# A hybrid decoder block: 14 of 24 gate tiles computed as pairs in one-level Strassen form

## The chip, the cores and the metric

The kernel runs on one core of a Trainium2 chip. Its parts are TensorE (PE, matrix products, which write to the accumulator memory PSUM), VectorE (DVE), ScalarE (ACT), GpSimd (POOL), and DMA engines; every transfer here is issued by SyncE (SP), which works through its list in order, as each engine does. The metric is the device time of one execution in microseconds (us), median of several runs. A profile, the "trace", was taken of one more execution.

## The reference

The work is one block of a decoder with D = 1024 features and 1024 tokens, 16 meta tokens prepended. Shortened:

```python
u = rms_norm(h, norm_mix)
qa, ka, va, qf, kf, vf, fl, xc, yc, gates = split(u @ w_in)
o_a = swa_sink_attention(qa, ka, va, ...)     # 8 heads, window of 128
o_f = forgetting_attention(qf, kf, vf, ...)   # 8 heads, causal, bias from cumulated log_f
o_c = rg_lru(causal_depthwise_conv(xc), ...) * gelu(yc)
g = sigmoid(gates).reshape(b, t, 3, D)
merged = g[..., 0, :] * (o_a @ w_branch[0]) + g[..., 1, :] * (o_f @ w_branch[1]) \
       + g[..., 2, :] * (o_c @ w_branch[2])
h = h + merged @ w_out
h = h + (silu(gate_ff) * up_ff) @ w_ffn_out   # gate_ff, up_ff from rms_norm(h) @ w_ffn_in
out = rms_norm(h)[16:]
```

`gates` has 3 x 1024 columns: 24 tiles of 128 features, each for 1024 tokens.

## The kernel before

All matrix products work on numbers split in two parts, `hi` and `lo` (`split`: ACT writes `hi`, DVE writes `lo` = source minus `hi`), and each product is three matmuls: hi*hi, hi*lo, lo*hi (`mm3`, L151). So one gate tile is 2 token halves x 8 blocks of 128 features x 3 = 48 matmuls with 512 columns. Its weights (512 KB) are loaded into a tile `wr` and split into `wh` and `wl`; each half's sum is copied from PSUM by ACT into a tile `z` and stored to the DRAM buffer `gz` (`gate`, L733).

The stages, in order of time:

1. Norm of the input, which leaves `uh` and `ul` (u, features in partitions), and the first projections.
2. The recurrence (`lru`, L359): 4 blocks of 128 channels, mostly long DVE and ACT operations and a scan. Beside it PE works on the remaining projections of the recurrence and on the values of both attentions (`values`, `mm_v`, results `vst`).
3. The attentions: first the sliding window (`swa_scores`, `swa_values`), then the forgetting one (`fox_scores`, `fox_values`). Scores go from PSUM (`sc`) through DVE (bias and maximum), ACT (exponential), DVE (reciprocal) and POOL (scaling; in the sliding window, every other tile on DVE, L596) to PE for transposes (`tr`), through `split` (`ph`, `pl`), and to PE again for the product with the values (`ob`).
4. The branch products (`mm_br`) of mixers A and C, from `o` tiles loaded from the DRAM buffer `osp`, with `gz` through a sigmoid (`sg`); then branch F; then the output projection.
5. The SwiGLU and its output, already in one-level Strassen form: 7 products instead of 8 on half-size blocks, with sums of blocks built by `combine` (L999) and `swiglu` (L943).

The order in stages 2 and 3 is made by `drive` (L237): a `side` generator (recurrence, or attention) yields after each piece, and between two pieces a `main` generator is stepped until its matmuls, at a written cost of 2.4 columns per ns and 3 ns each, add up to a gap: `LRU_GAP` = 3500 ns in the recurrence, `GAPS` = 850 ns in the sliding window, 480 ns in the forgetting attention. What is saved up is capped at `CREDIT` gaps. A scheduler then places the instructions of each engine. `main` beside the attentions holds the q and k projections and all 24 gates; what is left of them when the attention ends is done after it, alone. In time, the recurrence's last block runs beside the first projections of the attention.

Tiles live in pools on two sides of the on-chip memory; a pool that is opened after another was closed takes its place, and a tile waits for the last use of the one it lies on. Tiles of one tag rotate over a given number of buffers (`wh` and `wl` have two each).

## Time and profile before

| | |
|---|---|
| median of 3 runs | 1651.43 us (1650.43 to 1652.25) |
| the profiled execution | 1652.01 us, of which the span is 1650.2 |
| instructions in the span | 22634 |
| DMA | 242.48 MB, mean 147 GB/s |
| recurrence, from its first DVE operation to its last | 52.66 to 233 us of the span |
| attentions, first scores in a row to the last `ob` | about 240 to 734 us |
| gates after the attention | 734.41 to 777 us |

The span is one execution as the profiler saw it; the execution's own time is 1.8 us longer. PE is busy nearly all the time, but a matmul's busy time contains that of its neighbours, since they are pipelined. What PE really can do is read from how far apart matmuls start where nothing holds them up.

### The profile page before, as it was taken

To read this page: it belongs to the slowest core of one execution; us is meant where nothing else is said; L and a number is where in the kernel's file an instruction comes from. 1 tells how busy PE (TensorE), PEld (TensorE's weight loads), DVE (VectorE), ACT (ScalarE), POOL (GpSimd) and SP (SyncE) were. 2 spreads that over 40 slices of the span, in tenths; PEclk is the share of its full clock that TensorE was granted. 3 is DMA by queue.
4 is the path that set the end of the run, shared out by engine and by line. 5 is a ranking of instruction groups with operands and counts; after the bars stand their busy time and mean duration, and the time that the engine had idled before them with its cause. 6 is when DMAs were issued, how large, how long until landed. Compare 5 with 4: busy or idle time off the path is not lost.

```text
span 1650.2 us, 22634 instructions
## 1 busy us (share of the span) xinstructions
PE 1627.5 (99%) x8159; PEld 1372.3 (83%) x8159; DVE 1006.8 (61%) x1815; ACT 759.7 (46%) x1397; POOL 389.4 (24%) x322
## 2 busy tenths in 40 slices
PE   7999999999999999999999999999999999999998
PEld 6899978888888888888887888888888788888886
DVE  6566566555566666651338446977776777466554
ACT  6466466555555555542335443433333343355342
POOL 2000001011122221110224100267765667300000
PEclk9999999999999999999999999999999999999999
DMA  7222342223324142329747221344554444698632
GB/s 254 78 103 94 131 139 77 95 82 122 108 75 129 63 123 73 115 98 318 252 142 230 96 90 70 127 156 172 198 202 148 147 149 151 214 359 275 191 128 102
DMA packets 110880, 242.48 MB, mean 147 GB/s; under 512 B 11944, under 2 KB 23544, under 8 KB 110512
## 3 DMA queue, kind: packets, MB, share of 16 engines
q1 hardware_dynamic: 110768, 241.04, 43.0%
q8 instruction: 64, 1.05, 0.3%
q14 instruction: 48, 0.39, 0.1%
HBM read 163.45 MB, written 72.21 MB: 143 GB/s over the span
## 4 chain that ended last, share of the span: by engine, by line
PE 81%; DVE 6%; DMA 4%; POOL 3%; issue 3%; ACT 2%; SPq 0%; DVEq 0%; POOLq 0%; ACTq 0%
PE mm_w L151 27%; PE mm_s L151 7%; PE mm_br L151 6%; PE mm_wo L151 5%; PE mm_x L1147 4%; PE mm_v L151 4%; PE tr_s L151 4%; PE tr_y L1147 4%; PE sc_y L1147 4%; PE ob L547 4%; PE tr L558 3%; DMA wr<-w_fi_dram 2%; PE sc_s L151 2%; PE ob_x L1147 1%; PE mm_g L151 1%
## 5 line engine op out<-in xcount | busy, mean ns | idle before, releaser
L151 PE MATMUL mm_w<-uh,wh 128*128 128x512 f32 (+2 forms) x744 | 292.6, 393 | 0.0
L151 PE MATMUL mm_w<-uh,wl 128*128 128x512 f32 (+2 forms) x744 | 280.6, 377 | 0.0
L151 PE MATMUL mm_w<-ul,wh 128*128 128x512 f32 (+2 forms) x744 | 279.9, 376 | 0.0
L151 PEld LDWEIGHTS mm_w<-uh,wl 128*128 128x128 f32 x744 | 140.0, 188 | 25.7
L151 PEld LDWEIGHTS mm_w<-uh,wh 128*128 128x128 f32 x744 | 140.4, 189 | 12.8
L151 PEld LDWEIGHTS mm_w<-ul,wh 128*128 128x128 f32 x744 | 140.7, 189 | 11.7
L119 DVE TENSOR_TENSOR ab<-raw,ab 128x1024 fp32r<-128x1024 f32 x77 | 92.9, 1223 | 71.5 <-ACT ab L118 62.0
L118 ACT ACTIVATE wh<-wr 128x1024 fp32r<-128x1024 f32 (+1 forms) x84 | 72.0, 858 | 125.3 <-PE mm_w L151 52.3
L118 ACT ACTIVATE ab<-raw 128x1024 fp32r<-128x1024 f32 x77 | 80.8, 1059 | 95.0 <-PE ob_x L1147 21.4
L151 PE MATMUL mm_s<-pt,ar 128*128 128x512 f32 x492 | 118.8, 390 | 0.8 <-ACT c L954 0.7
L151 PE MATMUL mm_br<-o,wh 128*128 128x512 f32 x384 | 118.3, 389 | 0.0
L119 DVE TENSOR_TENSOR pl<-tr,ph 128x384 fp32r<-128x384 f32 (+2 forms) x160 | 87.4, 555 | 46.9 <-ACT ph L118 42.7
L151 PEld LDWEIGHTS mm_s<-pt,ar 128*128 128x128 f32 x492 | 92.0, 188 | 21.5 <-ACT c L968 1.3
L118 ACT ACTIVATE ph<-tr 128x384 fp32r<-128x384 f32 (+2 forms) x160 | 77.0, 486 | 52.9 <-PE tr L558 50.9
L119 DVE TENSOR_TENSOR wl<-wr,wh 128x1024 fp32r<-128x1024 f32 x45 | 55.8, 1241 | 73.4 <-ACT wh L118 73.1
L648 POOL TENSOR_SCALAR s<-s,sm 128x144 f32<-128x144 f32 (+3 forms) x64 | 48.8, 765 | 171.0 <-DVE sm L647 138.1
L151 PEld LDWEIGHTS mm_br<-o,wh 128*128 128x128 f32 x384 | 72.1, 188 | 14.8
L558 PE MATMUL tr<-ident,s 128*128 128x128 f32 x480 | 79.6, 274 | 1.2 <-POOL s L596 0.6
L151 PE MATMUL mm_wo<-woh,hl 128*128 128x512 f32 x256 | 79.1, 389 | 0.0
L151 PE MATMUL mm_br<-o,wl 128*128 128x512 f32 x192 | 75.2, 392 | 1.5 <-DVE wl L119 1.5
L558 PEld LDWEIGHTS tr<-ident,s 128*128 128x128 f32 x480 | 59.1, 140 | 18.3 <-DVE pl L119 3.4
L1147 PE MATMUL mm_x<-ab 128*128 128x512 f32 x297 | 72.7, 389 | 0.0
(258 smaller groups left out, 3651.9 us busy)
## 6 DMA issues: line engine op xcount, KB each, us to landing
wr<-w_in_dram SPq DMA_DIRECT2D x45, 512.0 KB, 3.6
wr<-w_fi_dram SPq DMA_DIRECT2D x44, 512.0 KB, 4.1
raw<-asp SPq DMA_DIRECT2D x77, 256.0 KB, 3.3
asp<-a SPq DMA_DIRECT2D x66, 256.0 KB, 2.8
gz<-z SPq DMA_DIRECT2D x48, 256.0 KB, 2.0
o<-osp SPq DMA_DIRECT2D x24, 512.0 KB, 5.9
sg<-gz SPq DMA_DIRECT2D x48, 256.0 KB, 3.5
fo<-w_fo_dram SPq DMA_DIRECT2D x22, 512.0 KB, 4.5
```

Of the source, the lines that this page charges most:

```text
L118: a = act.activation(hi, src, AF.Copy)
L119: i = dve.tensor_tensor(lo, src, f32(hi), ALU.subtract)
L151: pe.matmul(ps, a, b, start=first and i == 0, stop=i == n - 1, skip_group_check=not first)
L547: pe.matmul(ob[:, q0:q0 + b - a], vt[:, c], x[:, a:b], start=count == 0, stop=count == n_mm - 1, skip_group_check=True)
L558: pe.transpose(tb[:, col:col + P], src, ident)
L648: pool.tensor_scalar(s[:, :nk], s[:, :nk], den, 1.0, ALU.mult, ALU.mult)
L1147: pe.matmul(banks[x], a[:, 0, q], b[:, 1], start=first and j == 0 and c == 0, stop=j == NJ - 1 and c % 3 == 2, skip_group_check=True)
```

## The change

- Three gates stay plain and move into the recurrence's stage (`PLAIN`), one behind the values of the second set, two at the end. The recurrence's pieces come at shorter gaps (`LRU_GAP` 2200), and the projections of its last block move ahead of the values.
- A new stage follows the recurrence: `combine` builds four sums T1 to T4 of the quarters of u (`ub`: 2 feature halves x 2 token halves, so each quarter and each sum is two tiles of 128 x 1024), in the space that the recurrence leaves (`rt`, with three scratch tiles `fo` in `rf`).
- Seven pairs of gate tiles (`gate_pair`, `PAIRS`) are then computed in 7 products of 12 matmuls instead of 96 matmuls. Each pair needs 7 splits of 128 x 512, 4 sums of weight blocks, and 3 copies and 3 additions of partial results. Its tiles (`rg`) take the place of `rf`.
- Seven gates remain beside the attentions. `GAPS` are 290 and 345 ns, `CREDIT` is 30, and a gate can be interrupted by a q or k projection.
- In the sliding window all of the scaling is on POOL.
- The branch products run in the order A0, A1, C0, A2, C1, ... instead of A0, C0, A1, C1, ...
- `sub`, `add`, `product`, `operand` and `combine` move up in the file; `combine` takes its tiles as arguments.

```diff
-LRU_GAP = 3500.0
-GAPS = (850.0, 480.0)
-CREDIT = 8
+LRU_GAP = 2200.0
+GAPS = (290.0, 345.0)
+PLAIN, PAIRS = 3, 7
+CREDIT = 30
...
+    def combine(blocks, pair, temp):
+        b11, b21, b12, b22 = blocks
+        t3, t2, t1 = ([pair(i) for _ in range(2)] for i in (3, 2, 1))
+        room = lambda: temp().rearrange("p (k t) -> p k t", k=2)
+        v2 = []
+        for i in range(2):
+            v3 = room()
+            v2.append(room())
+            for v, x, y in zip((v3, v2[i]), b22[i], b12[i]):
+                sub(dve, v, f32(x), f32(y))
+            add(dve, v3, v3, v2[i])
+            for x, y in zip((v3, v2[i]), b11[i]):
+                add(dve, v2[i], x, f32(y))
+            split(*t2[i], v2[i])
+            split(*t3[i], v3)
+        def less_t2(t, b):
+            for i in range(2):
+                v = room()
+                sub(dve, v, f32(b[i][0]), v2[i])
+                add(dve, v, v, f32(b[i][1]))
+                last = split(*t[i], v)
+            return last
...
     def lru_main():
...
+        yield from proj(XC + 3, FULL, xs)
+        yield from proj(YC + 3, REAL, ys)
+        done.add(("lru", 3))
         yield from values(1, w_v1, 328)
...
-        yield from proj(XC + 3, FULL, xs)
-        yield from proj(YC + 3, REAL, ys)
-        done.add(("lru", 3))
+        yield from gate(gates.pop(0))
...
         yield from values(0, w_v0, 320)
+        for _ in range(PLAIN - 1):
+            yield from gate(gates.pop(0))
...
+        rt = ctxg.enter_context(tc.tile_pool(name="rt", bufs=1, side="right", reuse_waits="tile"))
+        with tc.tile_pool(name="rf", bufs=1, side="right", reuse_waits="tile") as rf:
+            ub = [[tuple(x[c][:, k:k + 2, (0 if c else NM):(0 if c else NM) + 512] for x in (uh, ul))
+                   for k in (k0, k0 + 2)] for c in range(2) for k0 in (0, 4)]
+            ub, _, rest = combine(ub, lambda i: [rt.tile([P, D], F32R, tag="t", bufs=16, name=nm("t"))
+                                                 .rearrange("p (k t) -> p k t", k=2) for _ in range(2)],
+                                  lambda: rf.tile([P, D], F32, tag="fo", bufs=3, name=nm("fo")))
+            ub.append(rest())
+    rg = ctxg.enter_context(tc.tile_pool(name="rg", bufs=1, side="right", reuse_waits="tile"))
+
+    def gate_pair(ja, jb, pl):
+        b11, b21, b22, t1, t2, t3, t4 = ub
...
+        product(p1, operand(wp, "wh", 2, a11), b11)
+        act.activation(c11, p1, AF.Copy)
+        product(p2, operand(wp, "wl", 2, a12), b21)
+        add(dve, c11, p2, c11)
+        dma(gz[ja, :, lo], c11)
+        sub(dve, a21, a11, a21)
+        sub(dve, s2, a22, a21)
+        product(p1, operand(rg, "ar", 3, s2), t2, False)
+        act.activation(c12, p1, AF.Copy)
+        add(dve, a11, s2, a11)
+        product(p5, operand(rg, "ar", 3, a11), t1)
+        act.activation(c22, p5, AF.Copy)
+        product(p1, operand(rg, "ar", 3, a21), t3, False)
+        add(dve, c22, p1, c22)
+        dma(gz[jb, :, hi], c22)
+        sub(dve, a12, a12, s2)
+        product(p5, operand(wp, "wh", 2, a12), b22, False)
+        add(dve, c12, p5, c12)
+        dma(gz[ja, :, hi], c12)
+        product(p1, operand(wp, "wl", 2, a22), t4, False)
+        act.activation(c21, p1, AF.Copy)
+        dma(gz[jb, :, lo], c21)
+
+    for i in range(PAIRS):
+        gate_pair(gates.pop(0), gates.pop(0), rg if i % 2 else wp)
+    ctxg.close()
...
-                (dve if jj % 2 else pool).tensor_scalar(s4[:, jj, lo:], ...)
+                pool.tensor_scalar(s4[:, jj, lo:], s4[:, jj, lo:], sm[:, 1, jj:jj + 1], 1.0, ALU.mult, ALU.mult)
...
-        todo = [(g, m) for m in range(8) for g in (0, 2)]
+        todo = [(0, 0), (0, 1)] + [(g, m + d) for m in range(8) for g, d in ((0, 2), (2, 0)) if m + d < 8]
```

How the change moves instructions is seen in the order that the built programs have, engine by engine. A row is line, operation, output<-inputs and shape; no times are in it.

First DVE behind the last values (`vst`). Before, the recurrence's last block (`g`, `q`, `x`, `y`, `xl`) alternates with the first k and q projections:

```order
L119 TENSOR_TENSOR wl_2109<-wr_2106,wh_2108 128x1024
L393 TENSOR_TENSOR g_1818<-g_1818,x_1803 128x1040
L396 SCALAR_TENSOR_TENSOR q_1849<-r_1817,q_1849 128x1040
L119 TENSOR_TENSOR k_1942<-mm_w_256_2007,k_1941 64x512
L397 TENSOR_TENSOR g_1818<-q_1849,g_1818 128x1040
L492 SCALAR_TENSOR_TENSOR q_2040<-mm_w_262_2048,q_2040 64x512
L400 SCALAR_TENSOR_TENSOR x_1856<-r_1817,g_1818 128x1040
L492 SCALAR_TENSOR_TENSOR q_2041<-mm_w_262_2048,q_2041 64x512
L401 SCALAR_TENSOR_TENSOR y_853<-x_1856,y_853 128x1024
L492 SCALAR_TENSOR_TENSOR q_2040<-mm_w_263_2077,q_2040 64x512
L119 TENSOR_TENSOR wl_2303<-wr_2300,wh_2302 128x1024
L119 TENSOR_TENSOR xl_1860<-y_853,xh_1859 128x1024
```

In the change the recurrence's operations are over by the last `vst`, and 26 operations of 128 x 1024 follow, the sums and splits of `combine` (`fo`, `t`). These are the last eight of them and what comes next, the first operand (`ar`) for a product that needs a sum of u:

```order
L370 TENSOR_TENSOR fo_2098<-fo_2098,ul_102 128x1024
L120 TENSOR_TENSOR t_2070<-fo_2098,t_2069 128x1024
L367 TENSOR_TENSOR fo_2107<-uh_99,fo_2072 128x1024
L370 TENSOR_TENSOR fo_2107<-fo_2107,ul_101 128x1024
L367 TENSOR_TENSOR fo_2112<-uh_99,fo_2083 128x1024
L120 TENSOR_TENSOR t_2104<-fo_2107,t_2103 128x1024
L370 TENSOR_TENSOR fo_2112<-fo_2112,ul_101 128x1024
L120 TENSOR_TENSOR t_2106<-fo_2112,t_2105 128x1024
L367 TENSOR_TENSOR s_293_2132<-wr_2124 128x512
L370 TENSOR_TENSOR c_2129<-sc_w_288_2127,c_2129 128x512
L370 TENSOR_TENSOR wr_2122<-s_293_2132,wr_2122 128x512
L120 TENSOR_TENSOR ar_2169<-s_293_2132,ar_2169 128x512
```

So the block of weights `s`, the addition into `c` and the operand `ar` of the first pair, which lie in `rg` on the space of `fo`, stand behind all of `combine`. On ACT the same stretch begins like this (`z` are copies of the plain gates' sums, `mm_w` their banks, `wh` and `wl` here the first pair's operands):

```order
L484 ACTIVATE z_1958<-mm_w_250_1933 128x512
L119 ACTIVATE wh_2134<-wr_2122 128x512
L484 ACTIVATE z_1986<-mm_w_252_1961 128x512
L119 ACTIVATE wl_2150<-wr_2122 128x512
L119 ACTIVATE t_2063<-fo_2072 128x1024
L119 ACTIVATE t_2059<-fo_2071 128x1024
L484 ACTIVATE z_2020<-mm_w_257_1995 128x512
L119 ACTIVATE t_2065<-fo_2083 128x1024
```

The first `hi` part of a sum (`t`) now stands behind copies of the plain gates' halves and behind the pair's `wh` and `wl`.

Second, SP behind the attention. Before, the loads of mixer C's `o` tiles and then of the first branch weights (`wb`) and gates (`sg`) alternate with the stores of the gates that PE does alone; two more of these come behind `wb`:

```order
L58 DMA gz<-z_7730 128x512
L58 DMA o_1431_7846<-osp 128x1024
L58 DMA o_1435_7850<-osp 128x1024
L58 DMA o_1432_7847<-osp 128x1024
L58 DMA gz<-z_7758 128x512
L58 DMA o_1436_7851<-osp 128x1024
L58 DMA wb_7876<-w_br_dram 128x512
L58 DMA sg_7878<-gz 128x512
L58 DMA sg_7879<-gz 128x512
L58 DMA wb_7882<-w_br_dram 128x512
L58 DMA gz<-z_7792 128x512
L58 DMA sg_7884<-gz 128x512
```

In the change only two stores of such gates are left here, `wb` comes behind the last of them and five more `o` loads:

```order
L59 DMA gz<-z_7918 128x512
L59 DMA o_1474_7970<-osp 128x1024
L59 DMA o_1478_7974<-osp 128x1024
L59 DMA o_1475_7971<-osp 128x1024
L59 DMA gz<-z_7946 128x512
L59 DMA o_1479_7975<-osp 128x1024
L59 DMA o_1476_7972<-osp 128x1024
L59 DMA o_1480_7976<-osp 128x1024
L59 DMA o_1477_7973<-osp 128x1024
L59 DMA o_1481_7977<-osp 128x1024
L59 DMA wb_8002<-w_br_dram 128x512
L59 DMA sg_8004<-gz 128x512
```

Third, PE in the sliding window. Before, matmuls of a gate (`mm_w`) stand in groups of three and four between transposes (`tr`) and products with the values (`ob`):

```order
L558 MATMUL tr_2279<-ident,s_2154 128x128 x3
L558 MATMUL tr_2310<-ident,s_2154 128x128 x4
L151 MATMUL mm_w_320_2372<-uh_100,wl_2303 128x512
L151 MATMUL mm_w_320_2372<-uh_100,wh_2302 128x512
L151 MATMUL mm_w_320_2372<-ul_102,wh_2302 128x512
L151 MATMUL mm_w_320_2372<-uh_100,wl_2303 128x512
L547 MATMUL ob_2278<-ph_2280,v_2117 128x128
L151 MATMUL mm_w_320_2372<-uh_100,wh_2302 128x512
L151 MATMUL mm_w_320_2372<-ul_102,wh_2302 128x512
L558 MATMUL tr_2333<-ident,s_2154 128x128
L547 MATMUL ob_2278<-pl_2281,v_2117 128x128
```

In the change fewer of them stand between the scores (`sc`) and the rest; from the first scores of the sliding window to the last `ob` of the forgetting attention, the order has 1342 matmuls `mm_w` of 512 columns before, and 660 in the change. From that last `ob` to the first `mm_br` it has 189 before and 105 in the change.

```order
L707 MATMUL sc_3771<-k_3057,q_3439 128x256
L670 MATMUL ob_3696<-pl_3726,v_3235 128x128
L708 MATMUL sc_3771<-k_3058,q_3439 128x256
L152 MATMUL mm_w_551_3753<-ul_101,wh_3749 128x512
L152 MATMUL mm_w_551_3753<-uh_99,wl_3750 128x512
L707 MATMUL sc_3788<-k_3057,q_3439 128x256
L708 MATMUL sc_3788<-k_3058,q_3439 128x256
L152 MATMUL mm_w_551_3753<-uh_99,wh_3749 128x512
L152 MATMUL mm_w_551_3753<-ul_101,wh_3749 128x512
L152 MATMUL mm_w_551_3753<-uh_99,wl_3750 128x512
L707 MATMUL sc_3805<-k_3057,q_3439 128x256
L708 MATMUL sc_3805<-k_3058,q_3439 128x256
```

More of the change, by code (lines that the diff above doesn't have):

```diff
@@ L418, in lru_side, with gate, zsink @@
             yield from lru(m, bdh, bdl)
+    gates = [8 * g + m for g in (0, 2, 1) for m in range(8)]
+    def gate(j):
+        def zsink(ps, n, t0):
+            zt = zp.tile([P, 512], F32, tag="z", bufs=2, name=nm("z"))
+            act.activation(zt, ps[:, :n], AF.Copy)
+            dma(gz[j, :, t0:t0 + n], zt)
+        yield from proj(GT + j, REAL, zsink)
     def lru_main():
@@ L747, in main @@
                     done.add(key)
+                    continue
+                part_of = part_of or gate(gates.pop(0))
+                cost = next(part_of, None)
+                if cost is None:
+                    part_of = None
                 else:
[L749 removed]
+                    yield cost
         drive(main(), side(), lambda: GAPS[mixer[0]])
```

121 lines of the change are left out of this document (51 added, 70 removed).

## The prediction

> **What bounds the kernel now.** I read the page first: busy shares, then the chain of waits that ended last.
>
> ```profile
> PE 1627.5 (99%) x8159; PEld 1372.3 (83%) x8159; DVE 1006.8 (61%) x1815; ACT 759.7 (46%) x1397; POOL 389.4 (24%) x322
> PE 81%; DVE 6%; DMA 4%; POOL 3%; issue 3%; ACT 2%; SPq 0%; DVEq 0%; POOLq 0%; ACTq 0%
> ```
>
> TensorE sets the end: it is busy 99% of the span and holds 81% of the chain. How much time a matmul really takes is read from that chain in order of time (start, length, what), where PE runs without a break:
>
> ```profile
> 734.41 42.88 PE mm_w L151 x189
> 777.30 86.83 PE mm_br L151 x383
> 1303.00 2.72 PE sc_s L151 x12
> ```
>
> 42.88 / 189 and 2.72 / 12 both give 0.227 us for a matmul of 512 columns; the first line is also the gates that PE does alone behind the attention, and `mm_br` follows them at once. A saved matmul is worth 0.227 us as long as PE has its next operands in time; where it has not, nothing of the saving is seen. So everything below is a comparison of what PE has left to do at a place with what the others need until then. The busy time by stages (start:end, length, then PE, its weight loads, DVE, ACT, POOL, the clock, the DMA share and GB/s) tells how much cover there is:
>
> ```profile
> 240.00:426.50 186.50, 185.38 (x1017) 156.75 (x1016) 108.29 (x290) 100.72 (x259) 22.47 (x35) 1.00 0.27 93
> 426.50:734.40 307.90, 306.85 (x1831) 266.06 (x1830) 195.31 (x620) 168.99 (x353) 64.61 (x77) 1.00 0.31 95
> 734.40:777.30 42.90, 42.90 (x191) 35.49 (x190) 5.11 (x7) 10.00 (x15) 0.00 (x0) 1.00 0.92 320
> ```
>
> Beside the attentions DVE is busy 304 of 494 us, so the gates there hide it easily. In the 43 us behind them the DMA is the busy one: 92%, 320 GB/s.
>
> **The change, part by part.** *Fewer matmuls.* Seven pairs need 84 instead of 96 matmuls each: 84 fewer, 84 x 0.227 = 19.0 us. This is the whole gain; nothing else is removed from PE. Within the pairs PE should run as in the SwiGLU's same products (2.72 us each, above): a pair is 19.0 us of PE, against 14 DVE operations of 128 x 512 at 0.60 (rows below), 8.4 us, and 10 on ACT at 0.63, 6.3 us. Hidden.
>
> *The sums of u.* The recorded order of DVE has 26 operations of 128 x 1024 behind the last `vst`, and the operand of the first pair's third product behind all of them. The SwiGLU's own sums show their price (start, length, engine; then one split on ACT and one of the values):
>
> ```profile
> 1046.96 0.69 DVE L119 TENSOR_TENSOR ar<-s,ar 128x512 fp32r<-128x512 f32 x1
> 1047.56 1.22 DVE L900 TENSOR_TENSOR fo<-pt,fo 128x1024 f32<-128x1024 f32 x1
> 1048.70 1.22 DVE L119 TENSOR_TENSOR pt<-fo,pt 128x1024 fp32r<-128x1024 f32 x1
> ...
> 1039.36 1.06 ACT L118 ACTIVATE pt<-fo 128x1024 fp32r<-128x1024 f32 x1 [4.11 <-DVE fo L903]
> ...
> 184.60 0.49 DVE L119 TENSOR_TENSOR vst<-mm_v,vst 128x320 fp32r<-128x320 f32 x1 [3.41 <-ACT vst L118]
> ```
>
> From start to start 1.14 us for 1024 columns, 0.60 for 512; ACT's half of a split takes 1.06. Count from the end of the last `mm_v`. PE then has two plain gates (96 matmuls) and the two products that need only u itself (24): 120 x 0.227 = 27.2 us. DVE needs about 1 us for the last `vst` (ACT's copy, then 0.49), 26 x 1.14 = 29.6, and seven operations of 512 among and behind them, 4.2: 34.8 us, were it never to wait. It waits, though. The pair's `wh` can be written only when the first plain gate's `wh` is free, after 48 matmuls, at 10.9; DVE stands before its half of it at 1 + 6 x 1.14 = 7.8, and ACT does `wh`, a copy, `wl` and the first sum's `hi` (some 3 us) before DVE has its first half of a sum, at about 14 instead of 9; that is some 4.6 lost. And four of the eight splits of sums have nothing of DVE's between the sum and its `lo`, so DVE stands for ACT's 1.06 to 1.2 each: 4.6. That makes 44.0, and PE, ready at 27.2, waits 17 us. Bounds: 7.6 if DVE never waits, 19 if its dependent operations take 1.22 instead of 1.14. I take 17, since buffers and order force the waits. Behind PE's third product stand all its later ones and the attention; nothing else can be issued.
>
> *Behind the attention.* PE has 105 matmuls there instead of 189, 23.8 us. SP's own queue in this stretch before, two groups of DMA issues (size, time to landing), and on ACT the last copy of a gate and the first split of a branch weight:
>
> ```profile
> 737.12 0.32 SPq L58 DMA_DIRECT2D osp<-pl  x1
> ...
> 738.03 0.40 SPq L58 DMA_DIRECT2D o<-osp  x1
> ...
> 761.69 0.32 SPq L58 DMA_DIRECT2D gz<-z  x1
> 762.05 1.41 SPq L58 DMA_DIRECT2D o<-osp  x3
> ...
> 767.97 0.44 SPq L58 DMA_DIRECT2D wb<-w_br_dram  x1
> ...
> o<-osp SPq DMA_DIRECT2D x18, 512.0 KB, 5.9
> wb<-w_br_dram SPq DMA_DIRECT2D x4, 256.0 KB, 5.3
> ...
> 771.94 0.60 ACT L736 ACTIVATE z<-mm_w 128x512 f32<-128x512 f32 x1 [4.84 <-PE mm_w L151]
> 774.37 0.63 ACT L118 ACTIVATE wh<-wb 128x512 fp32r<-128x512 f32 x1 [1.83 <-DMA wb<-w_br_dram]
> ```
>
> The loads start 3.6 us after the last `ob` (734.4) and the first `wb` is there at 774.3, 40 us after it; PE came at 777.1. With 23.8 us of cover, the same loads cannot be done. In the change's order SP first waits for the last plain gate's copy (24.4 with ACT's 0.6), issues its store (0.32), five more `o` loads at 0.47, and `wb`: 27.1. With 5.3 us to land and 0.63 for the split, PE starts at 33.1 instead of 23.8: a wait of 9.3. By the load instead: 16 x 0.524 + 5 x 0.262 of `gz` + 0.524 of `w_out` + 0.262 = 10.5 MB at 320 GB/s is 32.8, from 3.6 on, and 0.63: 37.0, a wait of 13.2. If `wb` lands in 2 us, 6.0. I take 9.5, near the queue's own walk. The order A0, A1 lets mixer C's tiles come 5.4 us later, but `wb` stands behind them all the same. The Trainium skill, "DMA: Bandwidth & Descriptors", section "Where 436 GB/s comes from", says that HBM transfers are bound by about 358 GB/s per core; an estimate by it is 29.3 us for these bytes and a wait of 9.7. This trace ran at 320 in this stretch.
>
> *A restart after a long wait.* At its start PE had idled, and its first matmuls came slowly:
>
> ```profile
> 15.90 0.43 PE L151 MATMUL mm_w<-uh,x1h 128*128 128x272 f32 x1
> ...
> 17.76 0.43 PE L151 MATMUL mm_w<-ul,x0h 128*128 128x272 f32 x1
> 17.99 0.43 PE L151 MATMUL mm_w<-uh,x0l 128*128 128x272 f32 x1
> ...
> 19.35 0.31 PE L151 MATMUL mm_w<-uh,x0l 128*128 128x272 f32 x1
> ...
> 19.87 0.29 PE L151 MATMUL mm_w<-uh,x0h 128*128 128x272 f32 x1
> 19.99 0.29 PE L151 MATMUL mm_w<-ul,x0h 128*128 128x272 f32 x1
> ```
>
> 0.23 apart until 19.35 and 0.12 from there: 3.45 us at half the pace, 1.7 lost. Whether a wait in the middle does the same no row shows, because there is none so long; 0 to 1.7 for each of the two new waits. I take 1.7, the only row of a PE that had stood long: 3.4. The Trainium skill's page "TensorE: Matmul & The Clock Gate", section "What's actually happening", says that after an idle window of about 3.4 us the array runs at half rate until it was busy as long again; by it the term stays, without it it is 0.
>
> *A denser attention.* From the first scores to the last `ob` the order has 660 wide `mm_w` instead of 1342: 154.6 us of cover go elsewhere, and 494 us become 340 if nothing stalls. DVE loses 15 of its splits of gate weights and half of the scaling (groups of DVE: count | busy, mean ns | idle before and what ended it; the first of the forgetting attention, the others of the sliding window; last a wait of the chain):
>
> ```profile
> L119 DVE TENSOR_TENSOR wl<-wr,wh 128x1024 fp32r<-128x1024 f32 x18 | 22.1, 1225 | 36.1 <-ACT wh L118 36.1
> L596 DVE TENSOR_SCALAR s<-s,sm 128x256 f32<-128x256 f32 x32 | 12.9, 442 | 0.5
> L119 DVE TENSOR_TENSOR pl<-tr,ph 128x512 fp32r<-128x512 f32 x15 | 10.4, 691 | 12.7 <-ACT ph L118 12.5
> L119 DVE TENSOR_TENSOR pl<-tr,ph 128x384 fp32r<-128x384 f32 x15 | 8.3, 553 | 10.5 <-ACT ph L118 10.5
> ...
> 236.04 4.71 DMA nb<-bss
> ```
>
> 304 - 18.4 - 12.9 = 272 us of 340, 80% instead of 61%. In the sliding window it is tightest: taking its wide `mm_w` from 654 to 250, by the order up to the forgetting attention's first scores (91.6 us), leaves about 95 us of the 186.5, and DVE keeps 108.3 - 12.9 - some 7 = 88. DVE's idle before the two `pl` forms, 23 us, was waiting for ACT and cost nothing while gates ran; PE meets part of it now. Bounds: -5 (the first bias now arrives during the pairs, and PE's wait of 4.71 for it goes) and +20 (most of those waits). POOL takes 32 more scalings of about 0.6 us and lengthens the path to the transposes. I take +5: DVE is nearly full, but not over.
>
> Sum, against the profiled execution: 1652.0 - 19.0 + 17 + 9.5 + 3.4 + 5 = 1667.9. Its time is 0.6 above the median, so 1667 us.
>
> **The rivals.** *The covers nearly hold* (faster or the same). One mechanism: DVE's and SP's queues run as fast as their bare durations, so PE waits 7.6 and 6.0, and attention gains the 4.71: 1651.4 - 19.0 + 7.6 + 6.0 + 0 = 1646, or 1641 with the gain. For it: DVE is idle 39% now. Against it: the order puts ACT's copies ahead of the first `hi`. It turns into no gain once the two waits pass 19 together. *The saving shows whole:* 1632. That needs DVE's 34.8 us of work to fit in 27.2; only if the recurrence's stage gives PE other work. *Attention becomes bound by DVE and ACT* (slower): the sliding window's 95 us turn into DVE's 88 plus most of its 23 of ACT waits, and the forgetting attention loses a little too, +20 in place of +5: 1682. It decides where the matmuls between two scores are shorter than DVE's path for one; for it, the 80%. That the change doesn't do what it says is excluded: the order has 84 matmuls fewer.
>
> **How the numbers follow.** Forecast 0.55 (1667, own range 1655 to 1678). Covers nearly hold 0.22 (1646; about 0.17 faster, 0.05 no change). Whole saving 0.08. Attention bound 0.15. A change of under 0.2%, 3.3 us, can't be told from none. Faster 0.25; same 0.08 (0.05, and 0.03 from the forecast's low end); slower 0.67. All terms at their low ends give 1651.4 - 19.0 + 7.6 + 6.0 - 5 = 1641, all at their high ends 1651.4 - 19.0 + 19 + 13.2 + 3.4 + 20 = 1688. The range 1642 to 1686 leaves out the whole saving and the outer ends.
>
> **What would show it.** In the trace of the changed kernel: one gap of PE of 8 to 19 us at the third product of the first pair, ended by DVE's `ar`, with combine's DVE rows running through it; a second of 6 to 13 before the first `mm_br`, ended by the DMA of `wb` or the split; matmuls about 0.45 apart just behind each, or not; seven pairs of 19.0 us without gaps; and the stage from the first scores to the last `ob` at 340 to 360 us with DVE near 80%. A first gap under 5 us, or `wb` there before PE, would make the forecast wrong; an attention of 365 us or more would make it too low.

## The result, and the profile after

The changed kernel takes 1696.98 us (median of 5 runs, 1696.15 to 1698.06) against 1650.43 of the kernel before in the same session (1647.79 to 1652.25): 1.0283 of its time, 95% interval 1.0268 to 1.0298. It is slower by 46.6 us, where the prediction had 16 and a range up to 1686. The profiled execution's span is 1695.1 us against 1650.2, so the trace shows 44.9 of it.

From the page of the changed kernel, busy shares and the chain by engine:

```profile
PE 1632.4 (96%) x8075; PEld 1361.7 (80%) x8075; DVE 1050.1 (62%) x1893; ACT 783.4 (46%) x1442; POOL 399.6 (24%) x354
PE 82%; DVE 7%; ACT 5%; issue 2%; DMA 2%; POOL 1%; SPq 0%; DVEq 0%; ACTq 0%; POOLq 0%
```

The 84 matmuls are gone (8159 to 8075). TensorE is busy 96% instead of 99%, and ACT and DVE hold 12% of the chain instead of 8%. Two of the places show as single gaps. The first, in PE's timeline (start, length, what, idle time before it and what ended it), is the third product of the first pair:

```profile
230.82 0.39 PE L152 MATMUL sc_w<-uh,wl 128*128 128x512 f32 x1
248.09 5.70 PE L152 MATMUL mm_w<-t,ar 128*128 128x512 f32 x12 [16.88 <-ACT ar L119]
253.62 2.88 PE L152 MATMUL tr_w<-t,ar 128*128 128x512 f32 x12
```

PE stands for 17 us, and the 12 matmuls behind the gap take 5.5 from start to start where the next 12 take 2.72. DVE runs through the sums of u for nearly the whole of it, from 206.35 to 246.77, with some waits for ACT's half of a split. Behind the gap the seven pairs follow each other every 19.04 us, without a wait. The second gap is in the chain in order of time:

```profile
786.12 23.84 PE mm_w L152 x105
809.99 0.04 issue
810.03 0.61 ACT z L484
810.65 0.32 SPq L59
...
813.60 9.20 DMA wb<-w_br_dram
822.82 0.64 ACT wh L119
823.50 11.66 PE mm_br L152 x43
```

The 23.8 us of gates end at 809.96, the first branch matmul comes 13.6 later, and what it waited for is `wb`. The attention lies between the two gaps. Busy time by stages, as in the prediction (start:end, length, PE, weight loads, DVE, ACT, POOL, clock, DMA share, GB/s), sliding window, forgetting attention, and the stretch behind:

```profile
402.00:532.40 130.40, 125.95 (x713) 98.64 (x713) 90.91 (x261) 88.04 (x247) 34.60 (x68) 1.00 0.21 67
532.40:785.90 253.50, 246.51 (x1515) 209.66 (x1514) 179.74 (x608) 150.61 (x327) 64.81 (x76) 0.99 0.30 92
785.90:823.50 37.60, 24.04 (x107) 19.58 (x106) 2.45 (x5) 5.58 (x10) 0.00 (x0) 0.87 0.92 334
```

384 us instead of the 345 forecast, and with DVE at 271 of 384 us, 70%, not 80%: neither it nor ACT is full. To see what was lost here, take the gate and projection matmuls away. The same stages with the `mm_w` alone (behind the length stands PE's busy time, with the number of matmuls), first the kernel before, then the changed one:

```profile
241.20:433.10 191.90, 167.58 (x637) 107.19 (x637) 14.12 (x22) 21.57 (x38) 1.00 0.27 90
433.10:734.10 301.00, 224.12 (x832) 137.05 (x832) 17.52 (x30) 26.98 (x50) 1.00 0.31 95
```

```profile
401.60:532.40 130.80, 74.90 (x299) 50.30 (x298) 15.49 (x24) 13.93 (x25) 1.00 0.21 67
532.40:785.80 253.40, 143.08 (x555) 90.85 (x554) 17.54 (x30) 20.02 (x38) 0.99 0.30 92
```

Of the `mm_w`, 192 are projections of k with 272 or 256 columns (0.12 us each, 23.1 together), the others have 512 (0.227). Before: 492.9 - 1277 x 0.2267 - 23.1 = 180 us are attention's *own time*, its own matmuls and every stall. After: 384.2 - 662 x 0.2267 - 23.1 = 211. Attention's own matmuls are the same, so 31 us of stalls came in. Less some 150, my estimate of what its scores, transposes and value products take where nothing holds them up, this is the "excess" that the expectations below speak of: 31 us before, 61 after. Only differences of it are used. Half of the 31 us show where PE loads the transposes' weights (group of weight loads: busy, mean ns | idle before, what ended it), before and after:

```profile
L558 PEld LDWEIGHTS tr<-ident,s 128*128 128x128 f32 x480 | 59.1, 140 | 18.3 <-DVE pl L119 3.4 <-POOL s L596 0.9 <-POOL s L648 0.7
```

```profile
L681 PEld LDWEIGHTS tr<-ident,s 128*128 128x128 f32 x480 | 56.4, 141 | 33.8 <-POOL s L719 13.7 <-POOL s L770 10.8 <-DVE pl L120 2.4
```

The transposes now wait for the scaled rows: 15.5 of the 31 us are in this group, 1.7 come from a stretch at half clock (last section), and the rest is spread over other groups. With the recurrence, which stalls 3.5 us more (see below), the sum is -19.0 (84 matmuls) + 17.0 and 2.8 (sums, slow matmuls behind) + 31 (attention) + 13.6 and 1.7 (branches, slow matmuls behind) + 3.5 (recurrence) = 50.6. Against it stand 2.8 us of waits of weight loads between 205 us and the first scores in a row of the kernel before, which are gone, and 3.2 us by which the rest from the SwiGLU's first sums on is shorter: 44.6 of 44.9.

### The profile page after: what moved, and what is told of

Same layout as the page of the kernel before. It is cut to its first block, busy times and chain, and to the rows that moved or that the text cites. A ratio compares the mean times of both kernels' runs of the same rounds, so it can differ in the third digit from the quotient of the medians.

```text
span 1695.1 us, 22730 instructions
## 1 busy us (share of the span) xinstructions
PE 1632.4 (96%) x8075; PEld 1361.7 (80%) x8075; DVE 1050.1 (62%) x1893; ACT 783.4 (46%) x1442; POOL 399.6 (24%) x354
## 4 chain that ended last, share of the span: by engine, by line
PE 82%; DVE 7%; ACT 5%; issue 2%; DMA 2%; POOL 1%; SPq 0%; DVEq 0%; ACTq 0%; POOLq 0%
PE mm_w L152 19%; PE mm_s L152 13%; PE tr_s L152 6%; PE mm_br L152 6%; PE mm_wo L152 5%; PE mm_x L1209 4%; PE tr_y L1209 4%; PE sc_y L1209 4%; PE tr L681 3%; PE sc_s L152 3%; PE ob L670 3%; PE tr_w L152 2%; PE mm_v L152 2%; PE ob_x L1209 1%; PE mm_g L152 1%
## 5 line engine op out<-in xcount | busy, mean ns | idle before, releaser
L152 PE MATMUL mm_w<-uh,wh 128*128 128x512 f32 (+2 forms) x576 | 213.6, 377 | 0.0
L152 PE MATMUL mm_w<-ul,wh 128*128 128x512 f32 (+2 forms) x548 | 203.3, 372 | 0.0
L152 PE MATMUL mm_w<-uh,wl 128*128 128x512 f32 (+2 forms) x520 | 192.9, 372 | 0.1
L152 PE MATMUL mm_br<-o,wh 128*128 128x512 f32 x384 | 119.6, 393 | 13.6 <-ACT wh L119 13.6
L119 ACT ACTIVATE wh<-wr 128x512 fp32r<-128x512 f32 (+1 forms) x84 | 65.9, 786 | 123.7 <-PE mm_w L152 43.9
L152 PEld LDWEIGHTS mm_w<-uh,wh 128*128 128x128 f32 x576 | 108.6, 189 | 13.8 <-ACT wh L119 0.6
L152 PEld LDWEIGHTS mm_w<-ul,wh 128*128 128x128 f32 x548 | 103.5, 189 | 12.0
L152 PEld LDWEIGHTS mm_w<-uh,wl 128*128 128x128 f32 x520 | 98.2, 189 | 14.3 <-DVE wl L120 0.9
L681 PE MATMUL tr<-ident,s 128*128 128x128 f32 x480 | 88.6, 283 | 8.1 <-POOL s L770 4.3
L681 PEld LDWEIGHTS tr<-ident,s 128*128 128x128 f32 x480 | 56.4, 141 | 33.8 <-POOL s L719 13.7
L120 DVE TENSOR_TENSOR ar<-wr,ar 128x512 fp32r<-128x512 f32 x56 | 52.5, 942 | 38.4 <-ACT ar L119 37.8
```

The source lines that it names most:

```text
L119: a = act.activation(hi, src, AF.Copy)
L120: i = dve.tensor_tensor(lo, src, f32(hi), ALU.subtract)
L152: pe.matmul(ps, a, b, start=first and i == 0, stop=i == n - 1, skip_group_check=not first)
L681: pe.transpose(tb[:, col:col + P], src, ident)
```

## The experiments

Times below are medians; every ratio is to the kernel before, run in the same session (1648.9 to 1650.5). The changed kernel stands at 1697.0.

### The scaling back on two engines

```diff
-                pool.tensor_scalar(s4[:, jj, lo:], ...)
+                (dve if jj % 2 else pool).tensor_scalar(s4[:, jj, lo:], ...)
```

> The changed kernel, with the scaling of the sliding window's rows shared by VectorE and GpSimd again as in the kernel before; all else as changed. Theory 'GpSimd's path': with all four scalings of a group on GpSimd the transposes wait longer for it (13.7 us of weight-load waits on that scaling in the changed kernel); the sliding-window stage (first scores to the forgetting scores, 130.8 us) falls to about 120 and the time by 8 to 12 us, to 1685-1689. Theory 'thin cover': the stage is short of other matmuls, whoever scales; it stays within 3 us of 130.8 and the time within 3 us of 1697. A rise would say that VectorE, not GpSimd, was the engine to be spared.

1695.44 us, 1.0273 (1.0256 to 1.0290), not to be told from the changed kernel's 1.0283. The transposes' weight loads in its profile:

```profile
L681 PEld LDWEIGHTS tr<-ident,s 128*128 128x128 f32 x480 | 56.6, 140 | 28.1 <-POOL s L771 10.6 <-POOL s L719 5.1 <-DVE pl L120 4.4
```

The waits for the sliding window's scaling fall from 13.7 to 5.1, yet the stage only goes from 130.8 to 127.6 us: of the 8.6 us that left this releaser, 2.9 came back on others in the same group, and more on the value products. GpSimd's path is a small part, 3 to 4 us in the trace and not clear of noise in the medians; it is not the main cause.

### More cover for the sums

```diff
-PLAIN, PAIRS = 3, 7
+PLAIN, PAIRS = 5, 6
```

> The changed kernel with two more plain gates between recurrence and pairs and one pair fewer (5 plain, 6 pairs, 7 beside attention as before): 96 more matmuls of 512 columns, 21.8 us of cover, and 12 products (2.7 us) more work in all. Theory 'VectorE's sums outlast the cover': the wait before the third product of the first pair falls from 17.0 us to under 1, the slow matmuls behind it (12 in 5.70 us) go back to 2.72, and the time falls by 17.0 + 2.9 - 2.7 = 17 us, to 1680 (1677 to 1683). Rival 'the wait hangs on something that comes with the pairs' (their weights from memory, room that the recurrence leaves): the wait stays over 10 us and the time rises by 2.7, to 1700.

1679.82 us, 1.0177 (1.0161 to 1.0193): 17.2 us less, as expected to the microsecond. The group of the products that use sums, 24 fewer with the pair that is gone, has no idle time before it and no slow matmul (389 ns each; 408 in the changed kernel):

```profile
L152 PE MATMUL mm_w<-t,ar 128*128 128x512 f32 x144 | 34.6, 389 | 0.0
```

So the first gap is DVE's sums outlasting the matmuls beside them; the rival, something that comes with the pairs, is out.

### The form alone undone

The pair stage is replaced by 14 plain gates in the same place.

```diff
-PLAIN, PAIRS = 3, 7
+PLAIN, PAIRS = 17, 0
...
-            ub, _, rest = combine(ub, ...)
-            ub.append(rest())
...
-        gate_pair(gates.pop(0), gates.pop(0), rg if i % 2 else wp)
+        pass
```

> The changed kernel with the Strassen form alone undone: the fourteen gates of the seven pairs are computed plainly in the same place between recurrence and attention, 7 gates beside attention as changed. 84 matmuls of 512 columns more (+19.05 us), no sums of inputs and so no wait of 17.0 us and no slow matmuls behind it (-2.9). Theory 'the form saved 19.05 and its wait cost 19.9': the time is 1696, within 3 us of the changed kernel, and all of the 45 us lost lies outside the form. Rival 'the pair stage delays something else too' (banks, room that is freed late, loads of q and k): the time falls by 5 us or more, to 1692 or less. Rival 'plain gates wait for their weights in such a row': over 1700.

1694.47 us, 1.0275 (1.0260 to 1.0290). The Strassen form as placed here gave nothing: what it saved on matmuls, its sums cost in one wait. So the 45 us by which this kernel too is slower than the kernel before lie in what was moved to make room for it.

### The branches' first weights ahead of the outputs

```diff
+        ahead = [fetch(*x, r3) for x in todo[:2]]
         for g, o in ((0, oA), (2, oC)):
             for k in range(4):
                 load_o(o, g, k)
-        ahead = [fetch(*x, r3) for x in todo[:2]]
```

> The changed kernel with the first two weights of the branches and their gates loaded ahead of the attention outputs instead of behind all sixteen of them; nothing else is moved. Theory 'bytes ahead of the weight': the first branch then waits only for the weight and the first eight output tiles (4.2 MB, 13 us at 320 GB/s, beside 23.8 us of gate matmuls); its wait of 13.7 us falls under 2, the slow start goes, and the time falls by 13 to 15 us, to 1682-1684. Rival 'paid in the next step': the second half of the outputs is then late for the fourth branch, and more than half of the 13.7 us comes back inside the branch stage: time 1688 or more. Rival 'the split of the weight on ScalarE waits for another reason': no change, 1697.

1688.69 us, 1.0234 (1.0219 to 1.0249): 8.3 us less. The first branch matmul follows the last gate at once (807.7), but its rows in PE's timeline show the next wait at the third step:

```profile
809.68 0.50 PE L152 MATMUL mm_br<-o,wh 128*128 128x512 f32 x1 [0.21 <-DMA o<-osp]
...
824.90 1.22 PE L152 MATMUL mm_br<-o,wh 128*128 128x512 f32 x2 [5.06 <-ACT wh L119]
```

The weight of the third step is now the one behind the rest of the outputs. 13.6 us and the slow start went, 5.1 and its slow matmuls came, as the rival "paid in the next step" had it: the bytes were late, not one transfer.

### Thirteen gates beside attention, then twenty-three

First fewer pairs, 4 instead of 7, so that 13 gates lie beside attention:

```diff
-GAPS = (290.0, 345.0)
-PLAIN, PAIRS = 3, 7
+GAPS = (560.0, 440.0)
+PLAIN, PAIRS = 3, 4
```

> The changed kernel with 4 pairs instead of 7 and so 13 instead of 7 plain gates beside attention, the gaps between its pieces raised to 560 and 440 so that as much is left behind attention as in the changed kernel (99 matmuls against 105). 57.1 us leave the pair stage and 62.3 us of gates come back beside attention. By the changed kernel attention lasts 61 us longer than its own matmuls priced one by one, by the kernel before 31. Theory 'thin cover': the excess goes back to 31-40, attention lasts 416-425 us (first scores to last output), and the time is 1672-1682. Theory 'fixed waits' (GpSimd's path, copies of q and k, lumps at each change of heads, which come however many gates lie beside): the excess stays at 55 or more, attention lasts 440 or more, and the time is 1697 to 1703.

1689.08 us, 1.0241 (1.0222 to 1.0261). The attention with `mm_w` alone:

```profile
343.50:777.30 433.80, 308.56 (x1147) 188.44 (x1146) 33.05 (x54) 40.95 (x75) 1.00 0.28 89
```

433.8 - 955 x 0.2267 - 23.1 = 194: between the two theories, 44 us of excess. More than half of the loss went with six gates. (Gates are counted as they are handed to attention's stage, with those that are left over behind it; in wide `mm_w` beside it, it is 955 here, 662 in the changed kernel and 1277 before.) The kernel with the three repairs, below, has the same order in attention and 189. In this one PE waited 2.4 us for one weight's split and 1.7 for copies of k, and behind the first its clock was at half for 3.4 us. So own times of one order differ by some 5 us, where a single transfer or split comes late.

Then all seven pairs are kept, and 16 gates computed a second time beside attention:

```diff
-GAPS = (290.0, 345.0)
+GAPS = (950.0, 520.0)
...
+    gates += [8 * g + m for g in (0, 2, 1) for m in range(8)][:16]
```

> The changed kernel, pairs and all, with 16 of the gates computed a second time beside attention, so that 23 lie there as in the kernel before (gaps 950 and 520, some 183 matmuls left behind attention). The second computing adds 16 x 10.9 = 174 us of matmuls and nothing that is needed. It tells how much of attention's excess over its own matmuls (61 us in the changed kernel, 44 with 13 gates, 31 in the kernel before) is the number of gates alone. Theory 'thin cover alone': the excess goes to 28-34 us, attention itself (first scores to last output) lasts some 495-505 us, and the time is 1697 + 174 - 31 - 15 (the wait for the branches, covered by the longer tail) = 1825. Theory 'part of it is the other edits' (scaling on GpSimd, larger credit, main loop by parts): the excess stays at 40 or more, the time is 1835 or more.

1835.41 us in one run. The same view:

```profile
402.50:917.70 515.20, 412.54 (x1543) 256.48 (x1543) 33.02 (x54) 51.05 (x92) 1.00 0.29 92
```

515.2 - 1351 x 0.2267 - 23.1 = 186: the excess is 36 us. In the changed kernel's own code 25 of the 31 us vanish when the gates, and the gaps that go with them, are there again. My 1825 was 10 too low, and the time alone would speak for the second theory: 5 for the excess, 3 for waits in the SwiGLU that came back, the rest not placed. The 36 lies just above the band that I had given to cover alone; the 5 us over the kernel before are within the spread of one order, and may also belong to the other edits. The next run puts one of these by itself.

### The scaling alone, in the kernel before

```diff
-                (dve if jj % 2 else pool).tensor_scalar(s4[:, jj, lo:], ...)
+                pool.tensor_scalar(s4[:, jj, lo:], ...)
```

> The kernel before with one edit of the change alone: all scaling of the sliding window's rows on GpSimd. With 23 gates beside attention the excess of attention over its matmuls is 31 us. Theory 'a longer path costs only where cover is thin': within 1 us of the kernel before, 1649-1651. Theory 'part of attention's loss is this edit whatever the cover' (with 23 gates computed beside attention in the changed kernel's own code, 5 us of excess are left over the kernel before): 2 to 5 us more, 1652-1654, all of it in the sliding stage.

1650.57 us, 1.0004 (0.9996 to 1.0013): no change; the sliding stage is 1.1 us longer. By the traces, the same edit costs 1 us under 23 gates and 3 to 4 under 7. That fits a longer path being paid where little else is there to run, though the medians do not tell either from nothing.

### The recurrence's old order

```diff
-LRU_GAP = 2200.0
+LRU_GAP = 3500.0
...
-        yield from proj(XC + 3, FULL, xs)
-        yield from proj(YC + 3, REAL, ys)
-        done.add(("lru", 3))
 
         yield from values(1, w_v1, 328)
...
+        yield from proj(XC + 3, FULL, xs)
+        yield from proj(YC + 3, REAL, ys)
+        done.add(("lru", 3))
```

> The changed kernel with the recurrence's stage as before but for the gate that lies in it: the fourth pair of projections behind the first values again, the gap between its pieces 3500 again. In the changed kernel the last values matmul came 19.9 us later than before, of which a gate (10.9) and earlier work of the recurrence (4.2) explain 15.1. Theory 'the new order makes the stall': the last values matmul comes 4 to 5 us earlier, at 199 to 200 us from the start, and as the pieces of the recurrence that are pushed back fill the cover behind it, the time falls by up to 5 us, to 1692. Rival 'the gate in the stage brings the stall (its weight is late)': no change there, and the time stays within 2 us of 1697. Rival 'pieces pushed back delay the sums': the wait before the third product of the first pair grows over 20 us and the time rises.

1727.44 us, 1.0475 (1.0459 to 1.0490): 30 us worse. The weight loads of the recurrence's matmuls between 84 and 205 us, kernel before, then changed kernel:

```profile
L151 PEld LDWEIGHTS sc<-xh,bdh 128*128 128x128 f32 x16 | 3.0, 188 | 0.8 <-ACT r L387 0.5
```

```profile
L152 PEld LDWEIGHTS sc<-xh,bdh 128*128 128x128 f32 x20 | 3.7, 188 | 3.0 <-ACT xh L119 2.7
```

Over all weight loads there, the idle stretches of 0.1 us or more come to 1.2 us before, 4.7 after and 2.1 with the old order, where the last values matmul comes at 196.6 instead of 203.7. So the dense order does cost that stall, but the recurrence's pieces that the old order leaves behind keep DVE from the sums:

```profile
233.59 2.33 DVE x L459
239.52 3.41 DVE fo L367 x3
...
278.15 5.60 PE mm_w L152 x12
```

The last scan runs at 233.6, the first sum at 239.5 instead of 206.4, and the wait before the third product is 48.4 us instead of 16.9. So the rival that I had listed last holds: pieces pushed back delay the sums.

### The repairs together

Five plain gates, three pairs, 13 gates beside attention, early weights, and the second half of mixer C's outputs behind the third weight:

```diff
+GAPS = (560.0, 440.0)
+PLAIN, PAIRS = 5, 3
+        ahead = [fetch(*x, r3) for x in todo[:2]]
+        for k in range(4):
+            load_o(oA, 0, k)
+        for k in range(2):
+            load_o(oC, 2, k)
...
+            if i == 0:
+                for k in range(2, 4):
+                    load_o(oC, 2, k)
```

> Three repairs at once: 5 plain gates ahead of 3 pairs (13 gates beside attention, gaps 560 and 440), and the branches' first weights and gates loaded ahead of the outputs, the second half of the second set of outputs behind the third weight. From the kernel with 4 pairs (1689.1): cover for the sums -17.0 - 2.9 + 2.7 for the pair that is gone, the wait for the branches and its slow start -15.4. If the repairs add up, 1657 (1653 to 1661), still above the kernel before: what remains is 8.2 us saved by three pairs against 13 of attention's excess and 5 in the recurrence. If over 1665, one of the repairs gives its gain back in another stage (the third and fourth branch's loads, above all); under 1650 would say that the covers were not the whole loss.

1654.80 us, 1.0038 (1.0023 to 1.0052). The repairs add up. With the scaling shared again and the gaps at 580 and 440:

> The kernel with the three repairs (5 plain gates, 3 pairs, early loads; 1654.8), with the sliding window's scaling shared by VectorE and GpSimd again and the gaps at 580 and 440, so that 87 instead of 99 matmuls lie behind attention. Theory 'what is left is cover': the scaling gives 1 to 4 us as in its own run, the gaps under 1: 1651 to 1654, still not under the kernel before. Under 1649 would make the pairs a gain when repaired; over 1656 would say that VectorE is the bound as soon as the gates are thicker.

1652.60 us, 1.0016 (1.0007 to 1.0025); attention's own time is 185 us. Its branch stage lasts 140.1 us against 133.2 before. With the recurrence's pieces thinner on top (`LRU_GAP` 2500):

> The last kernel (5 plain gates, 3 pairs, early loads, shared scaling; 1652.6) with the recurrence's gap at 2500 instead of 2200: its pieces come as thinly as the room before the sums allows, in the new order. Theory 'the recurrence's stall is the density of its pieces': of the 4.6 us by which the matmuls stand idle between 84 and 205 us from the start, 2 to 3.5 go, the sums begin a little later but stay under their 49 us of cover, and the time is 1649 to 1651: no gain over the kernel before (1649.3), and none lost. Rival 'the sums come late': a wait before the third product of the first pair, 1655 or more. Rival 'order, not density': no change, 1651.5-1653.5.

1663.70 us, 1.0095 (1.0079 to 1.0112). The idle stretches between 84 and 205 us go from 4.7 to 0.5 us, and a wait of 11.9 stands before the third product again. Density and the sums' start are one choice: the stall is the price of the start.

### Less behind attention

The kernel before, with the new branch order, early loads, and gaps of 900 and 510, so that 108 instead of 189 matmuls are left behind attention:

```diff
-GAPS = (850.0, 480.0)
+GAPS = (900.0, 510.0)
...
-        todo = [(g, m) for m in range(8) for g in (0, 2)]
+        todo = [(0, 0), (0, 1)] + [(g, m + d) for m in range(8) for g, d in ((0, 2), (2, 0)) if m + d < 8]
+        ahead = [fetch(*x, r3) for x in todo[:2]]
...
```

> The kernel before, with no pairs: only the branch stage takes the changed kernel's order and loads its first weights and gates ahead of the outputs (the second half of the second set behind the third weight), and the gaps go to 900 and 510, so that 108 instead of 189 gate matmuls are left behind attention. Theory 'cover is worth time wherever it lies': 18 us of gates (1.7 gates) come to lie beside attention instead of behind it, at 1.4 us a gate (from 44 to 31 us of excess over ten gates) that saves 2 us; the 3.2 us by which the last stage of matmuls was shorter in the changed kernel come too if they hang on the branches' order. Together 1644 to 1648 against 1649.4 of the kernel before. Rival 'the kernel before wastes nothing there': 1649-1651. Rival 'the shorter tail uncovers the loads': over 1652, with a wait before the first branch.

1655.62 us, 1.0030 (1.0020 to 1.0040): slower by 0.3%. Attention's own time is 183 us, no lower with more gates, and the branch stage is 2.6 us longer, with a wait of 1.74 us inside it and not ahead of it. So neither place had anything to give, and the shorter tail uncovered loads. The last two runs ask the same of the repaired kernel: the branches in an order that needs mixer C two steps later, and then one pair fewer.

```diff
-        todo = [(0, 0), (0, 1)] + [... ((0, 2), (2, 0)) ...]
+        todo = [(0, m) for m in range(4)] + [... ((0, 4), (2, 0)) ...]
```

> The kernel with 5 plain gates, 3 pairs, early loads and shared scaling (1652.6), with the branches in another order: the first four of the first mixer ahead of all of the third mixer's, whose outputs are loaded behind the weights of the third and fourth step. In that kernel the branch stage lasts 140.1 us against 133.2 in the kernel before, because its loads (the DMA is 90% busy from 760 to 835 us) are late for the third and fourth step. Theory 'waits are the whole loss': the branch stage goes to 134-136 and the time falls by 4 to 6 us, to 1646.5-1648.5, at or just under the kernel before (1649.3). Rival 'the DMA's bytes bound this stretch, whatever the order': 138 us or more, and the time stays at 1651 or more.

1651.38 us, 1.0009 (1.0000 to 1.0018). The branch stage is still 139.9 us. Stages from the last `ob` on, kernel before and this one:

```profile
734.40:777.30 42.90, 42.90 (x191) 35.49 (x190) 5.11 (x7) 10.00 (x15) 0.00 (x0) 1.00 0.92 320
777.30:835.00 57.70, 57.70 (x256) 47.76 (x256) 22.43 (x32) 19.89 (x34) 13.69 (x10) 1.00 0.72 240
```

```profile
754.90:800.00 45.10, 42.90 (x186) 33.89 (x184) 8.53 (x14) 11.83 (x19) 0.00 (x0) 1.00 0.93 331
800.00:835.00 35.00, 32.62 (x144) 27.00 (x145) 12.98 (x19) 12.58 (x21) 6.84 (x5) 1.00 0.84 285
```

Before, 27.6 MB move in the 100.6 us up to 835, and the DMA has room in the second part; here 24.9 MB in 80.1 us at 93% and 84%. The rival is right: bytes bound this stretch, and the order chose only which step waits.

```diff
-PLAIN, PAIRS = 5, 3
+PLAIN, PAIRS = 5, 2
-GAPS = (580.0, 440.0)
+GAPS = (650.0, 465.0)
```

> The last kernel with 2 pairs and 15 gates beside attention (gaps 650 and 465) instead of 3 and 13. One pair fewer is 2.7 us more of matmuls. If attention's own time, 185 us with 13 gates, still falls with more of them (180 in the kernel before with some 21), this gives back at most 1.5: the time is 1.2 to 2.7 above the kernel with 3 pairs. If it comes out at or under the kernel with 3 pairs, cover beside attention is worth more than 1.4 us a gate even at 13, and no number of pairs is a gain here.

1654.23 us, 1.0025 (1.0015 to 1.0035). 2.8 us over the kernel with three pairs; attention's own time is 186 us, no lower than the 185 with 13 gates. A pair is worth its 2.7 us there, and from 13 to 15 gates attention gains nothing more.

Attention's own time against the gates that lie beside it is then: 209 to 211 us with 7 (five kernels), 208 with 7 and shared scaling, 189 and 194 with 13, 185 with 13 and shared scaling, 186 with 15 and shared scaling, 186 with 23, 180 and 181 in the kernel before and that with the scaling alone, 183 in the run with less behind attention. Nothing that I ran beats the kernel before; the best kernel with pairs, three of them, is at 1.0009 of its time.

## Why the prediction was wrong

*Right in its sign, a third in its size.* It had 16 us where 46.6 came. By its steps:

*84 x 0.227 = 19.0 saved:* right. Removing the form alone gives it back, against the wait and slow matmuls that went with it, and the removal of one pair of three costs 2.8.

*The sums, 17 us (7.6 to 19):* right, 17.0. DVE's walk was forecast at 44.0 behind the last values matmul; from 203.9 to the first matmul at 248.1 it took 44.2. The releaser is named ACT's `ar`, not DVE's, since ACT's half stands behind DVE's last `s`. That the total fits so well is in part luck: DVE began the sums 2.5 us behind the values matmul and not 1, its operations of 1024 columns came 1.22 us apart and not 1.14, and it waited 6.9 us and not 9.2. (A pair has four copies on ACT, not three; the pairs hide that too.)

*Behind the attention, 9.5 (6.0 to 13.2):* too low, 13.6, just over the upper bound. I had two ways of counting and took SP's queue; the one by bytes, 10.5 MB at 320 GB/s, gave 13.2 and was the right one. The chain says so: SP was done at 813.56, 27.7 us behind the last `ob` where I had 27.1, but `wb` landed 9.2 later, and I had taken 5.3. The experiments say it again: whatever was loaded first, another transfer was late.

*The restart, 1.7 for each wait:* 2.8 and 1.7, so 4.5 for 3.4.

*A denser attention, +5 (-5 to +20):* this is the step that failed. It measured +31, over its upper bound, and 25 of these come and go with the number of gates beside it. The error has two parts. I asked whether DVE would be full, found 80%, and concluded that little would be lost. DVE came to 70%, ACT to 62%, neither was the bound, and 31 us were lost all the same: the path of one row of scores through DVE, ACT, DVE, POOL, PE, ACT and DVE back to PE is a chain, and what counts is how long PE's other work lasts against that chain, not how full its links are. (That the loss goes with the gates is measured; that the chain's length is the reason is my reading of the releasers, and no run shortened the chain alone by much.) The 23 us of DVE's waits for ACT that I called costless were a sign of the chain's length. And my bound took only DVE's waits on two forms of `pl`, not POOL's scaling, behind which 24.5 of the 33.8 us before the transposes stand. (The 340 us for the stage was off as well, by some 14 us: the order's first scores, from which I counted the matmuls, lie at 225.3 in the trace of before, not at the 240 from which I counted its 494 us; and the forgetting attention's first scores come at 433.0, not 426.5. The term in the sum does not hang on that.) The term's lower end misread a row: the 4.71 us of `nb` in the chain are a load, during which PE ran gates until 240.7 and then waited 0.5 us. There was no wait of 4.71 to be saved, here or in the rival at 1641.

*The recurrence:* left out, 3.5. The change there was read for what it brings forward, not for what its denser pieces do to PE.

*The rival "attention bound by DVE and ACT", 1682:* it had the right stage and the right direction, but not the mechanism, and its price of +20 was too low too. My text named "365 or more" as what would make the forecast too low; it was 384.

*Open:* the 5 us of attention's 31 that stay with 23 gates; and the 3.2 us by which the time from the SwiGLU's first sums on is shorter in the changed kernel (it came back in the run with 23 gates, and is 1 us or less in the kernel before with the branch order).

## What to carry to other kernels

When independent matmuls are interleaved with a latency chain, price the chain's exposure by what is left between its steps, not by how busy its engines are: here 662 wide matmuls instead of 1277 beside attention, some 13 gates' worth, went with 31 us of stalls at 70% or less of DVE and ACT, or 2.4 us a gate, while a gate that went into a pair saved only 1.4. Before work is taken out of a stretch, ask for everything that it covers: the gates behind attention covered some 10 MB of loads, those beside it the softmax, and those in the recurrence the sums. If queue and bytes give two answers for a late load, the later one was right here, where the DMA was 92% busy.

## What the hardware showed that I had not expected

Slow matmuls follow a wait in the middle of a kernel, not only at its start, and a short wait can be enough. The granted clock is the last but two of each row: behind the 16.9 us wait of the changed kernel, and behind the 5.06 us wait of the kernel with early weights:

```profile
248.00:254.00 6.00, 5.92 (x14) 4.34 (x15) 5.97 (x10) 3.02 (x7) 0.00 (x0) 0.54 0.74 237
```

```profile
824.90:830.50 5.60, 5.60 (x15) 4.35 (x16) 1.64 (x3) 3.07 (x5) 0.00 (x0) 0.56 0.90 321
```

Matmuls start 0.43 us apart instead of 0.227. Behind the waits of 5 us or more in the middle of these kernels this lasted 3.2 to 5.9 us (5.3 behind 48.4, 3.5 behind the 13.6 of the changed kernel), so such a wait costs 1.6 to 3.0 us on top, not in proportion to its length. One wait of 16.88 us, the same in five kernels, was followed by 5.6, 5.5, 5.3, 3.4 and 3.2 us of it.

Shorter waits go either way. The changed kernel's attention has one of 1.92 us, ended by POOL's scaling at 556.8, and half clock behind it:

```profile
557.30:560.80 3.50, 3.50 (x16) 3.03 (x14) 1.31 (x3) 1.72 (x5) 0.89 (x2) 0.51 0.00 0
```

The same 3.4 us at half clock began 0.5 to 1.8 us behind the end of waits of 1.51 us (23 gates), 1.72 (the recurrence's old order), 1.85 (three pairs, shared scaling) and 2.39 (13 gates), and none came behind 1.74 (less behind attention), 1.91 (more cover) and 2.56 (the branches in another order). So no length in this range decides. The Trainium skill, "TensorE: Matmul & The Clock Gate", section "What's actually happening", says that the array falls to half its clock after an idle window of about 3.4 us and that the window runs freely. That like waits are followed by different lengths agrees with a window that runs freely; that half clock came behind waits of 1.51 to 2.39 us does not agree with 3.4 us of idling, and the traces do not show what does decide.
